# Post norms of a two-layer decoder trunk: sums of squares spread by a product with ones, roots computed on every partition

## The chip, the cores and the metric

The kernel runs on one core of one Trainium2 chip. A core has TensorE (PE in the profile, with its weight loads shown apart as PEld), VectorE (DVE), ScalarE (ACT), GpSimd (POOL) and SyncE (SP, which here only issues transfers). The metric is the time of one execution on the device in microseconds (us). The kernel before takes 1883.55 us, the median of three runs that lie between 1883.47 and 1885.15 us.

## The reference

The model is a trunk of two layers over 512 tokens and 16 meta tokens, 1024 features wide, in float32. Each layer is a half-step SwiGLU FFN, a token mixer (gated linear attention in layer 0, sliding-window attention in layer 1), and a second half-step FFN. After the first layer one set of keys and values is made. Every sub-layer is normed on both sides:

```python
def rmsnorm(x, g):
    xf = x.astype(jnp.float32)
    y = xf * lax.rsqrt(jnp.mean(xf * xf, axis=-1, keepdims=True) + EPS)
    return (y * g.astype(jnp.float32)).astype(x.dtype)
...
    h = h + 0.5 * rmsnorm(swiglu(rmsnorm(h, g[0]), w_ffn_in[layer, 0], w_ffn_out[layer, 0]), g[1])
...
    h = h + rmsnorm(mix, g[3])
    h = h + 0.5 * rmsnorm(swiglu(rmsnorm(h, g[4]), w_ffn_in[layer, 1], w_ffn_out[layer, 1]), g[5])
```

The outer `rmsnorm` of each line, the one whose result is added to `h`, is the post norm. It needs, for each token, the root of the mean square over the 1024 features of the sub-layer's output.

## The kernel before, in words

Features lie on partitions and tokens on the free axis: `H` (the residual stream) and `Y` (a sub-layer's output) are 128 partitions x 8 feature tiles x 528 tokens. So the sum of squares of a token runs over the 8 tiles, which ACT and POOL add up elementwise (`square_into`, L436), and over the 128 partitions, which PE sums.

Tokens go in two groups: 272 and 256 in layer 0, 256 and 256 in layer 1. At the end of a sub-layer (`out_steps`, L660) the output products of the first group are issued for all eight feature tiles m, then its norm is started as a job (L754, `finish.run`), then the output products of the second group follow, and then its norm. The next sub-layer begins with `x_first` (L607): 96 products on the first group's operand tiles (four weight units, eight feature tiles, three products each), then 96 on the second group's. PE therefore has the second group's output products while the first group is normed, and the first group's input products while the second group is normed.

The norm of a group is `Residual.run` (L505):

- After a delay, `rstd` (L419) is called with DVE as its engine. `root` (L362) multiplies the sums tile by a single column of ones, one small product for each chunk of tokens and each sums tile (L368): four chunks of 68 tokens for 272, two chunks of 128 for 256. There are one or two sums tiles: the default `parts=(1, 2)` gives one for the first group and two for the second, and `l1f1` (the norm after the attention of layer 1) has two for both. The sums then lie with tokens on partitions, 68 x 4 or 128 x 2.
- Ten small DVE instructions (L376 to L390) make the inverse root by a bit trick and two Newton-like steps.
- L423 puts the roots on a diagonal, `dg`, by a multiplication of the identity with the roots (68 x 272 or 128 x 256). After the planner's delay, L431 multiplies ones by `dg`, which brings each token's root to all partitions, in PSUM tile `r`.
- For each feature tile k, DVE computes `t = y * r` (L519) and `h = t + h` (L520), and `nxt.build` (L465) and `nxt.sumsq` make the next sub-layer's operand tile (ACT L470, DVE L471) and its squares. With 256 tokens `t` is the second half of `r`'s bank; with 272 it is a PSUM bank of its own for each k.

Where there is no next sub-layer (`out`), the first group goes to `store` (L526) and the second to `turn` (L542). The norms so treated are eleven: both groups of `l0m`, `l0f1`, `kv`, `l1m` and `l1f1`, and the first group of `out`. In the profile `l0f1` and `l1f1` appear as `l0f` and `l1f`, and `out`'s second group (`turn`) is `st_out`.

The order of PE's instructions is written by hand; that of the other engines is made by the compiler's scheduler from program order. The program order comes from a small planner (`Flow`, L72): its clock advances with each product by an estimate (L177), and jobs ask with `yield` for the time after which they go on. The constant `DCHAIN` (3.0) stands for the DVE chain between the sums' product and the spreading product. The pre norm of the next sub-layer (`Operand.factors`, L481) uses the same `rstd` with POOL as its engine, and is not touched.

Large SBUF tiles (weights after their split, operands, hidden tiles, scratch) share one pool of 32 pair slots (`pair_tile`, L158); small ones lie in pool `sm`; all PSUM tiles share eight banks.

Of the kernel before, what the change touches and what calls it, by code (L numbers as in the profile page):

```python
# [9 lines left out]
F32 = mybir.dt.float32  # L10
F32R = mybir.dt.float32r
I32 = mybir.dt.int32
AF = mybir.ActivationFunctionType
ALU = mybir.AluOpType
AX = mybir.AxisListType

P = 128
D = 1024
# [9 lines left out]
RSQRT_MAGIC = float(0x5F3759DF)  # L28
# [23 lines left out]
LOW = 1.0  # L52
SQUARED = 1.0
SCALED = 2.2
LAG = 5
PERIOD = 3.2
SLOWER = 4.0
# [78 lines left out]
def trunk_kernel(ctx: ExitStack, tc, a, out, last_out):  # L136
    nc = tc.nc
    pe, act, dve, pool, sp = nc.tensor, nc.scalar, nc.vector, nc.gpsimd, nc.sync
# [12 lines left out]
    ones = cp.tile([P, P], F32, name="ones")  # L151
# [3 lines left out]
    def ps(name):  # L155
        return pp.tile([P, 512], F32, tag="ps", name=name)

    def pair_tile(name, dt=F32R):  # L158
        return hp.tile([P, 2, TOK], dt, tag="pair", name=name)
# [5 lines left out]
    def flat(t):  # L165
        return t.rearrange("p a t -> p (a t)")
# [5 lines left out]
    def mm(o, lhs, rhs, start=True, stop=True, onto=False, cost=None):  # L172
        inst = pe.matmul(o, lhs, rhs, start=start, stop=stop, skip_group_check=onto)  # L173
        n = 1
        for d in rhs.shape[1:]:
            n *= d
        flow.clock += cost or (n / 2400 if rhs.dtype == F32R else max(n / 600, 0.12))  # L177
        return inst
# [36 lines left out]
    live, limit, room = [0], [16], [Job(None)]  # L215
# [187 lines left out]
    def half_roots(sums, dim, name):  # L403
# [12 lines left out]
        dve.scalar_tensor_tensor(yy, zz, 0.75, yy, op0=ALU.add, op1=ALU.mult)  # L416
        return yy

    def rstd(sq, n, dim, half, name, eng=pool, more=0.0):  # L419
        yy = root(sq, n, dim, name, eng, half=half)  # L420
        c, nch = yy.shape
        dg = sm.tile([P, 272], F32, tag="dg", name=f"dg_{name}", bufs=2)
        eng.tensor_tensor(  # L423
            dg[:c, :n].rearrange("p (j c) -> p j c", c=c),
            ident[:c, :c].unsqueeze(1).to_broadcast([c, nch, c]),
            yy.unsqueeze(2).to_broadcast([c, nch, c]),
            op=ALU.mult,
        )
        yield (DCHAIN if eng is dve else CHAIN) + more
        r = ps(f"r_{name}")  # L430
        mm(r[:, :n], ones[:c, :], dg[:c, :n])  # L431
        return r
# [18 lines left out]
    class Operand:  # L451
# [29 lines left out]
        def factors(self, gi, eng=pool):  # L481
            if self.column is not None:
                o, n = self.groups[gi]
                yield FACT + (ADDED if self.parts[gi] == 1 else 0)
                root(self.accs[gi], n, D, f"{self.name}_{o}", eng, *self.column[gi])
                yield CHAIN
                return
            if self.rt is None:
                self.rt = sm.tile([P, TOK], F32, tag="R", name=f"R_{self.name}", bufs=2)
            o, n = self.groups[gi]  # L490
            yield FACT + (ADDED if self.parts[gi] == 1 else 0)
            r = yield from rstd(self.accs[gi], n, D, False, f"{self.name}_{o}", eng, gi * BEHIND if eng is dve else self.more)
            act.activation(self.rt[:, o : o + n], r[:, :n], AF.Copy)
# [5 lines left out]
    class Residual:  # L499
# [5 lines left out]
        def run(self, gi, g, sums):  # L505
            o, n = g
            nxt = self.nxt
            if self.turned(gi):
                self.turn(g, sums)
                return  # L510
            yield 1.8 + (ADDED if self.parts[gi] == 1 else 0)
            r = yield from rstd(sums, n, D, self.half, f"post_{self.name}{gi}", dve)
            if nxt is None:
                yield from self.store(gi, g, r)
                return
            for k in range(KD):
                h, y = H[:, k, o : o + n], Y[:, k, o : o + n]
                t = r[:, 256 : 256 + n] if n <= 256 else ps(f"t_{self.name}{gi}{k}")[:, :n]
                dve.tensor_tensor(t, y, r[:, :n], op=ALU.mult)  # L519
                dve.tensor_tensor(h, t, h, op=ALU.add)  # L520
                nxt.build(gi, k)
                nxt.sumsq(gi, k)
                yield 1.0
            nxt.rjob[gi] = flow.spawn(nxt.factors(gi), gi * BEHIND)

        def store(self, gi, g, r):  # L526
            o, n = g
            rb = r[:, :n].unsqueeze(1).to_broadcast([P, 2, n])
            for k in range(0, KD, 2):
                h, y = H[:, k : k + 2, o : o + n], Y[:, k : k + 2, o : o + n]  # L530
                t = ps(f"t_{self.name}{gi}{k}").rearrange("p (k n) -> p k n", n=n)
                dve.tensor_tensor(t, y, rb, op=ALU.mult)
                dve.tensor_tensor(h, t, h, op=ALU.add)
                sp.dma_start(out[k : k + 2, :, o - META : o - META + n].rearrange("k p n -> p k n"), h)
                yield 1.0
# [46 lines left out]
    def x_units(x, nu, groups, evac):  # L582
        late = []

        def drain(i, g, p):
            for job in x.rjob:
                yield job
            evac(i, g, p)

        raw = x.column is not None  # L590

        for i in range(nu):
            w = next_w()
            pst = [ps(f"x{used[0]}_{gi}") for gi in range(len(groups))]
            for k in range(KD):
                for g, p in zip(groups, pst):
                    mm3(p[:, : g[1]], w, k, x.tiles[k], g, k == 0, k == KD - 1)
            done_w()
            for g, p in zip(groups, pst):
                if raw or all(job.done for job in x.rjob):  # L600
                    evac(i, g, p)
                else:
                    late.append(flow.spawn(drain(i, g, p)))
        return late
# [337 lines left out]
    def gla(x, finish):  # L942
        set_ahead(10)
        with tc.tile_pool(name="gp", bufs=1) as gp:
# [81 lines left out]
            def core(h, before):  # L1026
# [105 lines left out]
                act.activation(onm, pm[:META, :256], AF.Identity, scale=f[:META, 4:5])  # L1132
                yield SCALED
                pm = ps(f"pm{h}_t")
# [109 lines left out]
    def swa(x, kv, finish):  # L1244
        kz, vt, dv, vmz = kv
        cap[0] = used[0] + 8
        with tc.tile_pool(name="ap", bufs=1) as ap:
# [19 lines left out]
            def evac(u, g, p):  # L1267
                o, n = g
                if qd[u // 2] is None:
                    qd[u // 2] = pair_tile(f"q{u}", F32)  # L1270
                act.activation(qd[u // 2][:, u % 2, o : o + n], p[:, :n], AF.Copy, scale=0.125)
# [139 lines left out]
            def attend(i, *after_jobs):  # L1411
                wait = [*after_jobs, *paces[-1:]]
                softs.append(flow.spawn(soft(i, wait)))
                paces.append(flow.spawn(pace(i, wait)))
                cores.append(flow.spawn(core(i)))
# [4 lines left out]
            for i in range(8):  # L1420
                attend(i, turns[i // 4], *cores[max(i - LAG, 0) : max(i - LAG + 1, 0)])
            x_units(x, 4, L1W, lambda i, g, p: evac(4 + i, g, p))
# [3 lines left out]
            for i in range(8, 16):  # L1426
                attend(i, turned, cores[i - LAG])
            flow.wait(*cores[:4])
# [186 lines left out]
```

## Time and profile before

| what | value |
|---|---|
| median of three runs | 1883.55 us |
| time of the profiled execution | 1884.85 us |
| its span (first to last instruction) | 1883.1 us |
| granted TensorE clock | 0.999 |
| DVE busy | 1397.0 us (74%), 2829 instructions |
| ACT busy | 1026.3 us (54%), 2311 instructions |
| POOL busy | 164.0 us (9%), 297 instructions |
| DMA, mean | 93 GB/s |

Times are microseconds unless marked ns. L173 is the helper that issues all products, so product groups are told apart by tile names: `st_post_...` are the sums of a post norm, `r_post_...` its spread roots, `dg_post_...` the diagonal; the same names without `post` belong to the pre norms. A product in float32 shows as two records for each matmul. In a timeline row the columns are start, duration, engine, line, operation, output and inputs, shapes and count; the bracket gives how long the engine was idle before, and what it waited for. In the chain of work that ended last, a row is start, length and what it consists of.

### The profile page before, as it was taken

What the parts mean: (1) busy time and instruction counts of PE and PEld (TensorE: products, weight loads), DVE (VectorE), ACT (ScalarE), POOL (GpSimd) and SP (SyncE); (2) the same over time, 40 slices, a digit from 0 to 9 for tenths busy, and PEclk for the clock granted to TensorE, in tenths of its full rate; (3) what the DMA queues carried; (4) which work ended last, traced back from release to release, by engine and by line L of the source; (5) the groups of instructions that cost most, each with busy time, mean ns of one, the idle gap of its engine ahead of it and who ended that gap; (6) DMA issues with size and microseconds to landing.
All of it is one profiled execution on the core that took longest, in us unless ns stands there. A gap on an engine that the chain in (4) does not pass through costs nothing.

```text
span 1883.1 us, 37216 instructions
## 1 busy us (share of the span) xinstructions
PE 1865.4 (99%) x14453; PEld 1783.3 (95%) x14453; DVE 1397.0 (74%) x2829; ACT 1026.3 (54%) x2311; POOL 164.0 (9%) x297
## 2 busy tenths in 40 slices
PE   8999999999999999999999999999999999999998
PEld 8999999999999999999999898989987898989898
DVE  6885858767564788585888886868766779868685
ACT  5653535654446566363574553535757855636364
POOL 2000000230001300000033000000320140000002
PEclk9999999999999999999999999999999999999999
DMA  4333233421123123232351223233421212333331
GB/s 166 96 97 105 88 110 94 140 68 57 62 63 113 46 90 106 91 101 91 110 166 46 73 88 111 92 113 98 136 74 52 68 46 73 96 107 101 103 114 60
DMA packets 102273, 174.70 MB, mean 93 GB/s; under 512 B 11856, under 2 KB 24016, under 8 KB 102096
## 3 DMA queue, kind: packets, MB, share of 16 engines
q1 hardware_dynamic: 101520, 171.67, 29.0%
q8 instruction: 113, 1.85, 0.4%
q10 hardware_dynamic: 576, 0.65, 0.1%
q14 instruction: 64, 0.52, 0.1%
HBM read 169.66 MB, written 2.10 MB: 91 GB/s over the span
## 4 chain that ended last, share of the span: by engine, by line
PE 88%; DVE 7%; ACT 3%; issue 1%; DMA 0%; POOL 0%; SPq 0%; DVEq 0%; ACTq 0%; POOLq 0%
PE y L173 30%; PE a L173 19%; PE x L173 19%; PE c L173 8%; PE d L173 5%; DVE raw L262 1%; ACT w_s L256 1%; PE o L173 1%; DVE w_s L257 1%; PE e L173 1%; DVE w L257 1%; DVE w L238 1%; PE po L173 1%; ACT s L1348 0%; ACT Y L1348 0%
## 5 line engine op out<-in xcount | busy, mean ns | idle before, releaser
L257 DVE TENSOR_TENSOR w_s<-raw,w_s 128x512 fp32r<-128x512 f32 x288 | 193.9, 691 | 130.3 <-ACT w_s L256 128.7
L173 PE MATMUL y<-hidl0f,w 128*128 128x256 f32 (+1 forms) x2112 | 262.0, 285 | 1.1 <-DVE hidl0f L449 0.9
L173 PEld LDWEIGHTS y<-hidl0f,w 128*128 128x128 f32 x2112 | 259.0, 188 | 2.2 <-DVE hidl0f L449 1.5
L238 DVE TENSOR_TENSOR w<-raw,w 128x512 fp32r<-128x512 f32 x376 | 236.1, 659 | 30.7 <-ACT w L237 28.5
L256 ACT ACTIVATE w_s<-raw 128x512 fp32r<-128x512 f32 x288 | 175.1, 628 | 151.4 <-DVE raw L262 138.5
L173 PE MATMUL y<-hidl1f,w 128*128 128x512 f32 (+1 forms) x1344 | 251.1, 346 | 0.3 <-DVE hidl1f L935 0.2
L173 PEld LDWEIGHTS y<-hidl1f,w 128*128 128x128 f32 x1344 | 212.4, 188 | 35.1 <-DVE hidl1f L935 1.6
L237 ACT ACTIVATE w<-raw 128x512 fp32r<-128x512 f32 x376 | 206.4, 586 | 39.1 <-PE y L173 29.3
L262 DVE TENSOR_TENSOR raw<-raw,raw 128x512 f32<-128x512 f32 x288 | 198.3, 688 | 5.5
L444 POOL TENSOR_TENSOR acc_post<-acc_post,sq_post 128x256 f32<-128x256 f32 (+1 forms) x77 | 63.1, 820 | 1541.5 <-ACT sq_post L443 1540.7
L257 DVE TENSOR_TENSOR w<-raw,w 128x512 fp32r<-128x512 f32 x216 | 148.6, 688 | 29.9 <-ACT w L256 29.1
L256 ACT ACTIVATE w<-raw 128x512 fp32r<-128x512 f32 x216 | 134.0, 621 | 41.5 <-PE y L173 41.2
L173 PE MATMUL x<-x_l0m,w 128*128 128x272 f32 (+1 forms) x1152 | 152.1, 288 | 0.0
L173 PEld LDWEIGHTS x<-x_l0m,w 128*128 128x128 f32 x1152 | 143.4, 188 | 2.7 <-issue 1.7
L699 DVE TENSOR_TENSOR Y<-y,Y 128x256 f32<-128x256 f32 (+2 forms) x175 | 81.9, 474 | 71.9 <-PE y L173 71.4
L173 PE MATMUL a<-zl0f_t,w_s 128*128 128x264 f32 x864 | 117.2, 285 | 0.0
L173 PE MATMUL a<-zl1f_t,w_s 128*128 128x256 f32 x864 | 114.3, 281 | 0.8 <-ACT c L910 0.7
L173 PEld LDWEIGHTS a<-zl0f_t,w_s 128*128 128x128 f32 x864 | 110.0, 188 | 0.3
L173 PEld LDWEIGHTS a<-zl1f_t,w_s 128*128 128x128 f32 x864 | 107.3, 188 | 2.6 <-ACT c L910 2.3
L173 PE MATMUL x<-x_l0f,w 128*128 128x256 f32 (+1 forms) x768 | 99.4, 289 | 7.4 <-ACT w L237 6.2
L173 PEld LDWEIGHTS x<-x_l0f,w 128*128 128x128 f32 x768 | 96.3, 191 | 8.5 <-ACT w L237 6.2
L173 PE MATMUL x<-x_l1f,w 128*128 128x256 f32 (+1 forms) x576 | 93.0, 320 | 0.0
(514 smaller groups left out, 3215.7 us busy)
## 6 DMA issues: line engine op xcount, KB each, us to landing
raw<-in_w_in SPq DMA_DIRECT2D x352, 256.0 KB, 2.9
raw<-in_w_out SPq DMA_DIRECT2D x96, 256.0 KB, 3.3
raw<-in_w_last SPq DMA_DIRECT2D x48, 256.0 KB, 3.1
raw<-in_gla_in SPq DMA_DIRECT2D x48, 256.0 KB, 3.0
raw<-in_w_out SPq DMA_DIRECT2D x64, 128.0 KB, 2.9
raw<-in_gla_out SPq DMA_DIRECT2D x16, 256.0 KB, 2.8
raw<-in_w_q SPq DMA_DIRECT2D x16, 256.0 KB, 3.6
raw<-in_swa_out SPq DMA_DIRECT2D x16, 256.0 KB, 2.9
```

Of the source, the lines that this page charges most:

```text
L173: inst = pe.matmul(o, lhs, rhs, start=start, stop=stop, skip_group_check=onto)
L237: act.activation(w[:, 0, :m], raw[:, :m], AF.Copy)
L238: dve.tensor_tensor(w[:, 1, :m], raw[:, :m], w[:, 0, :m].bitcast(F32), op=ALU.subtract)
L256: act.activation(w[:, 0, :512], src, AF.Copy)
L257: dve.tensor_tensor(w[:, 1, :512], src, w[:, 0, :512].bitcast(F32), op=ALU.subtract)
L262: dve.tensor_tensor(dst, dst, src, op=ALU.add)
L444: pool.tensor_tensor(sums[0][:, :n], sums[0][:, :n], t[:, :n], op=ALU.add)
L699: dve.tensor_tensor(y, p[:, :n], y, op=ALU.add)
```

## The change

A new function, `spread`, takes the place of `rstd` in the post norms. It multiplies a full 128 x 128 tile of ones by each sums tile whole, so that the total of each token arrives on all 128 partitions at once. The ten DVE instructions then run on 128 partitions x 256 or 272 tokens instead of 128 x 2 or 68 x 4. The first writes back to the sums' PSUM bank `st`; the others use three stretches of a pair tile (`roots_...`) taken from the 32 slots. The diagonal and the product that spread it are gone. The sums' bank then serves as `t`, for 272 tokens too, and the roots are read from SBUF. The planner's delay for the chain is `SPREAD` (4.4) in the place of `DCHAIN` (3.0), and comes after the whole chain is issued.

```diff
+SPREAD = 4.4
...
+    def spread(sq, n, half, name):
+        st = ps(f"st_{name}")[:, :n]
+        for i, t in enumerate(sq):
+            mm(st, ones, t[:, :n], i == 0, i == len(sq) - 1)
+        room = flat(pair_tile(f"roots_{name}", F32))
+        yy, zz, ww = (room[:, i * 272 : i * 272 + n] for i in range(3))
+        last = (-0.25, 0.75) if half else (-0.5, 1.5)
+        dve.tensor_scalar(st, st, 1.0 / D, 1e-6, op0=ALU.mult, op1=ALU.add)
+        dve.tensor_scalar(yy.bitcast(I32), st.bitcast(I32), -0.5, RSQRT_MAGIC, op0=ALU.mult, op1=ALU.add)
+        dve.tensor_tensor(zz, yy, yy, op=ALU.mult)
+        dve.tensor_tensor(zz, zz, st, op=ALU.mult)
+        dve.tensor_scalar(ww, zz, 0.375, -1.25, op0=ALU.mult, op1=ALU.add)
+        dve.tensor_tensor(ww, ww, zz, op=ALU.mult)
+        dve.scalar_tensor_tensor(yy, ww, 1.875, yy, op0=ALU.add, op1=ALU.mult)
+        dve.tensor_tensor(zz, yy, yy, op=ALU.mult)
+        dve.scalar_tensor_tensor(zz, zz, last[0], st, op0=ALU.mult, op1=ALU.mult)
+        dve.scalar_tensor_tensor(yy, zz, last[1], yy, op0=ALU.add, op1=ALU.mult)
+        return yy, st
...
-            r = yield from rstd(sums, n, D, self.half, f"post_{self.name}{gi}", dve)
+            r, t = spread(sums, n, self.half, f"post_{self.name}{gi}")
+            yield SPREAD
...
-                t = r[:, 256 : 256 + n] if n <= 256 else ps(f"t_{self.name}{gi}{k}")[:, :n]
-                dve.tensor_tensor(t, y, r[:, :n], op=ALU.mult)
+                dve.tensor_tensor(t, y, r, op=ALU.mult)
...
-            rb = r[:, :n].unsqueeze(1).to_broadcast([P, 2, n])
+            rb = r.unsqueeze(1).to_broadcast([P, 2, n])
```

## The prediction

> **What bounds the kernel now.** I read the page first, then the list of who waited for whom on PE, then the chain of waits at the norms, then the DVE timeline there.
>
> ```profile
> span 1883.1 us, 37216 instructions
> ...
> PE 1865.4 (99%) x14453; PEld 1783.3 (95%) x14453; DVE 1397.0 (74%) x2829; ACT 1026.3 (54%) x2311; POOL 164.0 (9%) x297
> ...
> PE 88%; DVE 7%; ACT 3%; issue 1%; DMA 0%; POOL 0%; SPq 0%; DVEq 0%; ACTq 0%; POOLq 0%
> ```
>
> PE is idle for 18 us in 1883 and holds 88% of the chain. So time is won by giving PE less work, and lost wherever PE has to wait for an operand. The next list shows that a post norm hardly makes it wait so far:
>
> ```profile
> PE st_post_l1f L173 <- ACT acc_post L440: 0.9, 1, 0.9
> PE r_post_l1m L173 <- DVE dg_post_l1m L423: 0.7, 1, 0.7
> ```
>
> The chain of waits prices each piece of PE work in a norm. Columns: start, length, what.
>
> ```profile
> 362.01 0.43 PE st_post_l0m L173 x8
> ...
> 366.13 0.46 PE r_post_l0m L173 x2
> ...
> 986.56 0.79 PE st_post_kv L173 x8
> 987.35 1.62 PE x L173 x12
> ...
> 991.02 0.43 PE r_post_kv L173 x2
> ...
> 1860.05 0.34 PE st_post_out L173 x4
> ...
> 1864.04 0.43 PE r_post_out L173 x2
> ...
> 624.93 0.66 PE r_post_l0f L173 x2
> ```
>
> The reader sees that these pieces stand in PE's stream between dense products: PE pays for all of them.
>
> **The change part by part. PE.** The old spreading product has ones as weights and 256 or 272 columns in float32. The new sums' product has the same weights, size and type, so each costs what `r` costs: 0.43 us for 256, 0.46 for 272. With one sums tile the new product simply takes the place of `r`, and the small products go; with two, two new products stand against small ones and `r`.
>
> - First groups of 272, one tile (`l0m`, `l0f1`, `kv`): 3 x 0.43 = 1.3 us less.
> - First groups of 256, one tile (`l1m`, `out`): 2 x 0.34 = 0.7 us less.
> - Two tiles (the second groups of five norms, and the first of `l1f1`): 0.79 + 0.43 - 2 x 0.43 = 0.36 each, 6 x 0.36 = 2.1 us less.
>
> Together 4.1 us, all on PE's stream. I see no term of its own for the weights, since `r` has the same ones.
>
> Two waits for the diagonal go with it: 0.7 us at `l1m`, and 0.66 - 0.43 = 0.2 at `l0f1`: 0.9 us. The 0.9 us at `l1f1` is for squares that come late from ACT; I leave it where it is.
>
> **The DVE chain.** Before and after are to be compared from the sums' arrival to the first use of the root.
>
> ```profile
> 987.38 0.16 DVE L376 TENSOR_SCALAR av_post_kv<-st_post_kv 128x2 f32<-128x2 f32 x1 [0.29 <-PE st_post_kv L173]
> ...
> 989.42 0.43 DVE L423 TENSOR_TENSOR dg_post_kv<-ident,yv_post_kv 128x256 f32<-128x256 f32 x1
> 991.49 0.43 DVE L519 TENSOR_TENSOR r_post_kv<-Y,r_post_kv 128x256 f32<-128x256 f32 x1 [1.64 <-PE r_post_kv L173]
> 991.96 0.42 DVE L520 TENSOR_TENSOR H<-r_post_kv,H 128x256 f32<-128x256 f32 x1
> ```
>
> Before: 991.49 - 987.38 = 4.1 us, of which DVE waits 1.64 for the spread. After: ten wide instructions, one behind the other. No wide `TENSOR_SCALAR` of this kind is in the trace. From below each could cost the 0.16 us of L376, from above the 0.47 us from L519 to the dependent L520. I take 0.46 for all ten, since L519 and L520 have the width and either place of the operands: 4.6 us, and about 4.8 for 272. So a second group's root comes about 0.5 us later than before, not 2.5, because the trip over PE is saved. In return DVE is occupied all the time.
>
> In a first group the old chain shares DVE with the evictions of `y` and with POOL:
>
> ```profile
> 968.69 0.16 DVE L376 TENSOR_SCALAR av_post_kv<-st_post_kv 68x4 f32<-68x4 f32 x1
> 969.15 0.42 DVE L699 TENSOR_TENSOR Y<-y,Y 128x256 f32<-128x256 f32 x1
> ...
> 970.26 0.66 DVE L387 SCALAR_TENSOR_TENSOR yv_post_kv<-wv_post_kv,yv_post_kv 68x4 f32<-68x4 f32 x1
> ...
> 971.96 0.41 DVE L699 TENSOR_TENSOR Y<-y,Y 128x256 f32<-128x256 f32 x1
> 972.86 0.45 DVE L519 TENSOR_TENSOR t_kv<-Y,r_post_kv 128x272 f32<-128x272 f32 x1 [0.48 <-PE r_post_kv L173]
> ```
> ```profile
> 970.17 0.74 POOL L444 TENSOR_TENSOR acc_post<-acc_post,sq_post 128x256 f32<-128x256 f32 x1 [3.82 <-ACT sq_post L443]
> ```
>
> L387 takes 0.66 us where its neighbours take 0.16, and it ends with POOL's addition (970.17 + 0.74 = 970.91): a DVE instruction that comes during one waits it out. The Trainium skill (SBUF — State Buffer, Who interferes with whom) says that a DVE instruction with two SBUF inputs shares a read port with GpSimd, and whoever starts first holds it for the whole instruction; it speaks against a chain made ten times as wide, and the row agrees. I count one such hold of 0.5 us: 4.8 + 2 x 0.46 + 0.5 = 6.2 us against 972.86 - 968.69 = 4.2, so 2.0 us later. The cover is the second group's output products, which last until 982.43 in `kv` (row further down), so a first group's operands are still in time. But DVE passes on to the chain behind what it cannot make up: 0 to 1.5 us, as it is idle only 0.29 us ahead of `kv`'s second chain. I take the whole 1.5 at `kv`, 0.5 at `l1m` and nothing at `l1f1`.
>
> **Where PE will wait.** The second group's operands must be there when the first group's 96 input products are done, and PE now gets there 0.36 us sooner. The tightest places:
>
> ```profile
> 1365.31 0.15 DVE L376 TENSOR_SCALAR av_post_l1m<-st_post_l1m 128x2 f32<-128x2 f32 x1
> 1365.38 0.68 DVE L238 TENSOR_TENSOR w<-raw,w 128x512 fp32r<-128x512 f32 x1
> ...
> 1366.72 0.68 DVE L238 TENSOR_TENSOR w<-raw,w 128x512 fp32r<-128x512 f32 x1
> ...
> 1370.00 0.43 DVE L519 TENSOR_TENSOR r_post_l1m<-Y,r_post_l1m 128x256 f32<-128x256 f32 x1 [0.79 <-PE r_post_l1m L173]
> ...
> 1371.73 0.47 DVE L471 SCALAR_TENSOR_TENSOR x_l1m<-H,vec,x_l1m 128x256 fp32r<-128x256 f32 x1
> ...
> 1374.14 0.66 ACT L1271 ACTIVATE q<-x 128x256 f32<-128x256 f32 x2
> ```
> ```profile
> 1533.98 11.32 PE x L173 x96
> ```
> ```profile
> 1543.74 0.48 DVE L471 SCALAR_TENSOR_TENSOR x_l1f<-H,vec,x_l1f 128x256 fp32r<-128x256 f32 x1
> ```
>
> - `l1m`: ACT reads the first group's products at 1374.14, so PE turns to the second group about then. Its first operand is ready at 1372.20: 1.9 us to spare. After: PE comes 0.36 + 0.7 = 1.1 us sooner; three weight splits of 0.68 us stand in the chain (the first and the last above), and no idle time is left for them, so the operand comes 4.6 + 2.0 - (1370.00 - 1365.31) = 1.9 us later, and 0.5 more from the first group. PE waits 1.1 + 1.9 + 0.5 - 1.9 = 1.6 us.
> - `l1f1`: the last of the eight operands is ready at 1544.22, and PE needs it at 1533.98 + 7/8 x 11.32 = 1543.89: nothing to spare. 0.36 + 0.5 = 0.9 us of wait.
> - `kv`: rows below. At 991.46 there are 96 - 33 - 12 - 12 = 39 products of the first group left; at 7.37 / 60 = 0.123 us each PE reaches the second group at 996.3. The operand is ready at 993.79: 2.5 us to spare, of which 0.36 + 0.5 + 1.5 are used up. I allow 0.1 us for this and the two like it (`l0m`, `l0f1`), and up to 1 us each for the range.
>
> ```profile
> 982.43 4.13 PE x L173 x33
> ...
> 989.40 1.62 PE x L173 x12
> ...
> 991.46 7.37 PE x L173 x60
> ```
> ```profile
> 993.22 0.57 DVE L471 SCALAR_TENSOR_TENSOR x_kv<-H,vec,x_kv 128x256 fp32r<-128x256 f32 x1
> ```
>
> That makes 2.6 us of new waits; 0 if the scheduler puts the chain ahead of other DVE work, about 8 if it puts it behind.
>
> **Sum.** -4.1 - 0.9 + 2.6 = -2.4 us. The profiled execution takes 1884.85 us and its span 1883.1; it lies 1.3 us above the median of the three runs. So 1882.4 for an execution like it, and **1881.1** for the median.
>
> What I cost at nothing: `out`'s chain and store (DVE, hidden under the last output products); the roots read from SBUF instead of PSUM in L519 (one SBUF and one PSUM operand before, two SBUF operands after, exposed to POOL as above); the PSUM banks, of which the norm now needs one instead of one and eight passing ones.
>
> **The rivals.**
>
> *Full gain.* DVE's order adapts and PE never waits anew: -4.1 - 0.9 = -5.0, so 1878.5. For it: PE stands still for only 0.7 us at `l1m` today. Against it: the two places above are at their limit. Chance 0.25.
>
> *No change, through the pre norm.* POOL's root for the next operand runs beside the second group's chain, and wide DVE instructions hold it.
>
> ```profile
> 386.52 0.64 POOL L423 TENSOR_TENSOR dg_l0m<-ident,yv_l0m 68x272 f32<-68x272 f32 x1
> ...
> 389.46 0.62 PE L173 MATMUL r_l0m<-dg_l0m,ones 68*128 68x272 f32 x2
> ```
>
> Its diagonal is ready at 387.16, and PE asks for it at 389.46: 2.3 us to spare. Beyond that PE waits in order. If each of some ten POOL steps waited for one 0.46 us instruction, 4.6 us would be lost, 2.3 of them on PE; in one or two norms that eats the forecast's gain: about 1883.5. Against it: only part of POOL's root overlaps the chain. The Trainium skill (SBUF — State Buffer, Who interferes with whom) has the two sides block each other fully; it is the mechanism of this rival. Chance 0.1.
>
> *Slower, through the pair slots.* The chain's scratch comes from the 32 pair slots, and stays in use until the last k. Slots already run out:
>
> ```profile
> ACT w L256 <- PE y L173: 41.2, 26, 3.3
> ...
> ACT w L237 <- PE y L173: 29.3, 23, 2.2
> ```
>
> ACT waits for output products before it can write a split weight, up to 3.3 us at a time, because these free the slots. If the chain finds none, it waits as long; 3.3 + 0.9 us of delay against 1.9 to 2.5 to spare leaves 2 us of PE wait for each of five second groups: -5.0 + 10 = +5, so 1888.5. It decides the sign from 5 us of waits on. Against it: each output unit frees slots, and no wait of a norm's operand on a slot stands out in the trace. Chance 0.2.
>
> **How the numbers follow.** Forecast 0.45 (1880 to 1883.5 alone), full gain 0.25, pre norm 0.1, slots 0.2. 0.2% (3.8 us) is about what a measurement of this kernel can tell from no change: faster means under 1879.8, slower over 1887.3. The full gain falls below, and of the forecast a small part: 0.3. Of the slots' rival most lies above: 0.18. The rest, 0.52, is within. The range reaches from the full gain, 1878, to 1887, in the lower part of the slots' rival.
>
> **What would show it.** `st_post` pieces of 0.43 us for one tile and 0.86 for two, no `r_post`, no `dg_post`; ten chain instructions of about 0.42 us; PE's busy time some 4 us smaller; waits of PE on `x_l1m` and `x_l1f` of 1 to 2 us. Wrong would be: a wide float32 product that costs more than `r` did; PE waits at `l0m`, `l0f1` or `kv` of over 1 us; DVE or ACT waiting for a slot between a norm's sums and its chain; a changed order that moves time in the attention between 1390 and 1505 us, where I predict none.

## The result, and the profile after

The changed kernel takes 1899.44 us (median of five runs, 1898.76 to 1900.55) against 1883.55 us before: a ratio of 1.0082, with a 95% interval of 1.0071 to 1.0093. It is 15.9 us slower, where the prediction had 2.4 us faster. The profiled execution took 1899.72 us. In the changed kernel lines up to L418 stand one later than before, and those behind `spread` 21 later: the multiplication by the roots, L519, is L540; the addition L520 is L541; the operand's L471 is L492; GpSimd's addition L444 is L465; the eviction L699 is L720. The ten instructions of the wide chain are L428 to L437.

From the page of the changed kernel, the lines that answer to those shown of before:

```profile
span 1897.9 us, 37056 instructions
...
PE 1866.3 (98%) x14385; PEld 1780.6 (94%) x14385; DVE 1437.2 (76%) x2818; ACT 1028.7 (54%) x2311; POOL 175.6 (9%) x297
...
PE 72%; DVE 19%; ACT 5%; issue 2%; POOL 0%; DMA 0%; DVEq 0%; SPq 0%; POOLq 0%; ACTq 0%
```

PE is idle for 31.6 us instead of 17.7, its busy time has not fallen by the 4 us of the prediction, and DVE's share of the chain that ended last has gone from 7% to 19%. Whom PE waited for (us in total, times, longest):

```profile
PE x L174 <- ACT x_l0f L491: 2.6, 2, 2.0
PE x L174 <- ACT x_l0m L491: 2.4, 1, 2.4
...
PE x L174 <- DVE x_l1f L492: 1.7, 1, 1.7
PE x L174 <- ACT x_l1m L491: 1.5, 1, 1.5
PE x L174 <- ACT x_l1f L491: 1.4, 1, 1.4
```

All are operands of second groups, at `l0m`, `l0f1`, `l1m` and `l1f1`; together they are 9.6 us. The diagonals are gone from the list, as intended.

The granted TensorE clock adds to the two longest of these waits. It is 1.00 in nearly all of the trace, but 0.50 for 3.4 us from 403.3 us on, right behind the wait of 2.4 us at `l0m`, and for 3.4 us again from 638.8 us on, behind the one of 2.0 us at `l0f1`. Two windows at `l0m` (stretch, its length, PE's busy time and products, granted clock, DMA share, GB/s):

```profile
404.00:406.00 2.00, 2.00 (x12) 0.50 0.50 142
416.00:418.00 2.00, 2.00 (x19) 1.00 0.16 42
```

In the slow stretches the 128x256 products start every 0.213 us instead of every 0.118, and there are 16 of them in each: 16 x 0.095 = 1.5 us, 3.0 us together. PE counts as busy in them, which is part of the reason why its busy time has not fallen. The mean granted clock is 0.997 to 0.998 in all five executions, and 0.999 or 1.000 in nearly all of those of the kernel before; the profiled one of before has a single such stretch next to a norm, at 1505.9 us in `l1f1`. The waits of 1.4 to 1.7 us at `l1m` and `l1f1` are not followed by one. What a wait must be for it, no run here separates.

To see where the time came from, I take the first start of each norm's sums product (`st_post_...`) in the two traces. The difference from one to the next is what the stretch between them cost: the norm, and the products up to the next norm.

| stretch that begins with the norm | change's cost in the trace, us | predicted, us |
|---|---|---|
| before the first norm | +1.4 | 0 |
| `l0m` | +4.4 | -0.8 and some wait |
| `l0f1` | +4.6 | -1.0 and some wait |
| `kv` | +0.8 | -0.8 and some wait |
| `l1m` | +0.5 | -1.4 + 1.6 |
| `l1f1` | +2.6 | -0.7 + 0.9 |
| `out`, first group | +0.5 | -0.3 |

(The 1.4 us ahead of the first norm lie at the start of the program, before the first changed instruction. In the experiments below this stretch differs from before by -0.8 to +0.8 us.)

The cause shows in single instructions. First the kernel before, then the changed one, each beside two additions of GpSimd:

```profile
389.50 1.80 POOL L444 TENSOR_TENSOR acc_l0m<-acc_l0m,sq_l0m 128x256 f32<-128x256 f32 x2 [0.74 <-ACT sq_l0m L443]
389.73 0.42 DVE L519 TENSOR_TENSOR r_post_l0m<-Y,r_post_l0m 128x256 f32<-128x256 f32 x1
```
```profile
394.24 1.80 POOL L465 TENSOR_TENSOR acc_l0m<-acc_l0m,sq_l0m 128x256 f32<-128x256 f32 x2 [1.61 <-ACT sq_l0m L464]
394.49 0.97 DVE L540 TENSOR_TENSOR st_post_l0m<-Y,roots_post_l0m 128x256 f32<-128x256 f32 x1
395.38 0.95 DVE L492 SCALAR_TENSOR_TENSOR x_l0m<-H,vec,x_l0m 128x256 fp32r<-128x256 f32 x1
```

With the roots in PSUM the multiplication takes its 0.42 us in the middle of an addition (389.50 to 390.41). With the roots in SBUF it starts in the middle of one (394.24 to 395.17), and ends 0.3 us behind it: 0.97 us. This is no single case: of the 80 multiplications in the changed kernel, 37 start while a GpSimd instruction still runs for 0.1 us or more, and they take 0.72 us in the mean and up to 1.03; the other 43 take 0.43. Before, 47 start so, and none takes more than 0.44. The next instruction, the operand's L492, which had two SBUF operands before as well, is held by the second addition. The groups of all sixteen multiplications of a norm (busy time, mean ns), in the changed kernel:

```profile
L540 DVE TENSOR_TENSOR st_post_l0f<-Y,roots_post_l0f 128x272 f32<-128x272 f32 (+1 forms) x16 | 9.8, 610 | 0.3
...
L540 DVE TENSOR_TENSOR st_post_l1m<-Y,roots_post_l1m 128x256 f32<-128x256 f32 x16 | 9.3, 582 | 0.4
L540 DVE TENSOR_TENSOR st_post_kv<-Y,roots_post_kv 128x272 f32<-128x272 f32 (+1 forms) x16 | 9.2, 574 | 0.3
...
L540 DVE TENSOR_TENSOR st_post_l1f<-Y,roots_post_l1f 128x256 f32<-128x256 f32 x16 | 8.7, 542 | 0.2
L540 DVE TENSOR_TENSOR st_post_l0m<-Y,roots_post_l0m 128x272 f32<-128x272 f32 (+1 forms) x16 | 8.5, 534 | 0.3
```

and one of them before:

```profile
L519 DVE TENSOR_TENSOR r_post_l1m<-Y,r_post_l1m 128x256 f32<-128x256 f32 x16 | 6.8, 425 | 1.9 <-PE r_post_l1m L173 1.6
```

Together they take 45.5 us, where 80 at about 0.425 would take 34. What that does to a norm, at `l0m`'s second group in the changed kernel (DVE's timeline, then PE's):

```profile
384.57 0.42 DVE L428 TENSOR_SCALAR st_post_l0m<-st_post_l0m 128x256 f32<-128x256 f32 x1
...
389.02 0.43 DVE L540 TENSOR_TENSOR st_post_l0m<-Y,roots_post_l0m 128x256 f32<-128x256 f32 x1
...
405.20 0.95 DVE L492 SCALAR_TENSOR_TENSOR x_l0m<-H,vec,x_l0m 128x256 fp32r<-128x256 f32 x1
```
```profile
402.79 6.47 PE L174 MATMUL x<-x_l0m,w 128*128 128x256 f32 x39 [2.44 <-ACT x_l0m L491]
```

The chain itself is as predicted: 389.02 - 384.57 = 4.45 us for ten instructions (predicted 4.6). But DVE only gets to it at 384.57, because it is still busy with the first group, and from the first multiplication to the end of the last operand it needs 17 us.

### The profile page after: what moved, and what is told of

It is laid out like the page before. It is cut to its first block, busy times and chain, and to the rows that moved or that the text cites. A ratio compares the mean times of both kernels' runs of the same rounds, so it can differ in the third digit from the quotient of the medians.

```text
span 1897.9 us, 37056 instructions
## 1 busy us (share of the span) xinstructions
PE 1866.3 (98%) x14385; PEld 1780.6 (94%) x14385; DVE 1437.2 (76%) x2818; ACT 1028.7 (54%) x2311; POOL 175.6 (9%) x297
## 4 chain that ended last, share of the span: by engine, by line
PE 72%; DVE 19%; ACT 5%; issue 2%; POOL 0%; DMA 0%; DVEq 0%; SPq 0%; POOLq 0%; ACTq 0%
PE y L174 27%; PE a L174 17%; PE x L174 11%; PE c L174 7%; PE d L174 4%; DVE raw L263 2%; ACT w_s L257 2%; DVE w_s L258 2%; DVE w L258 2%; DVE H L541 1%; DVE w L239 1%; PE o L174 1%; PE e L174 1%; PE po L174 1%; DVE hidl1f L956 1%
## 5 line engine op out<-in xcount | busy, mean ns | idle before, releaser
L465 POOL TENSOR_TENSOR acc_post<-acc_post,sq_post 128x256 f32<-128x256 f32 (+1 forms) x77 | 65.9, 855 | 1530.6 <-ACT sq_post L464 1528.1
L720 DVE TENSOR_TENSOR Y<-y,Y 128x256 f32<-128x256 f32 (+2 forms) x175 | 81.7, 473 | 67.6 <-PE y L174 67.3
L174 PE MATMUL x<-x_l0f,w 128*128 128x256 f32 (+1 forms) x768 | 101.9, 293 | 11.1 <-ACT w L238 6.0
```

The costliest lines, as they stand in the source:

```text
L465: pool.tensor_tensor(sums[0][:, :n], sums[0][:, :n], t[:, :n], op=ALU.add)
L720: dve.tensor_tensor(y, p[:, :n], y, op=ALU.add)
```

## The experiments

**Theory P**: GpSimd's additions hold the DVE instructions that now read two SBUF operands, the 80 multiplications above all. **Theory Q**: the wide chain occupies DVE about 2 us longer per norm, and what follows is late for that. Times are medians; ratios are to the kernel before, run on the same chip, with a 95% interval. The experiments are numbered, and "the ninth kernel" is that of experiment 9. Times by stretch are taken as in the table above, against the kernel before.

**1. Roots back in PSUM.**

```diff
-        dve.scalar_tensor_tensor(yy, zz, last[1], yy, op0=ALU.add, op1=ALU.mult)
-        return yy, st
+        rr = bank[:, 256:512] if n <= 256 else ps(f"rr_{name}")[:, :n]
+        dve.scalar_tensor_tensor(rr, zz, last[1], yy, op0=ALU.add, op1=ALU.mult)
+        return rr, st
```

> The changed kernel, but the last instruction of the chain writes the roots to PSUM, so that the multiplication by the roots again reads one SBUF and one PSUM operand; nothing else differs. Theory P (the multiplication with two SBUF operands is held by GpSimd's additions: 80 of them took 45.5 us instead of 34.2): they fall back to 0.42-0.45 us each, 11 us of DVE go, and the kernel comes to 1886 to 1890 us. Theory Q (the wide chain keeps DVE occupied 2 us longer per norm, and later work of the norm is late for that): at most 3 us come back, 1896 us or more. If both share the loss: about 1892.

1892.04 us, ratio 1.0043 [1.0028, 1.0057]. Half comes back: the case of both sharing. But the edit also moved the order on DVE, which the compiler makes. At `l0m` in the changed kernel the evictions of the second group's `y` stand spread through the first group's chain (364.18, 366.30, 368.84 us); here all but the first stand behind it. DVE's timeline of this kernel, then PE's:

```profile
362.87 0.42 DVE L722 TENSOR_TENSOR Y<-y,Y 128x256 f32<-128x256 f32 x1
370.65 0.41 DVE L722 TENSOR_TENSOR Y<-y,Y 128x256 f32<-128x256 f32 x1
```
```profile
377.13 3.65 PE L174 MATMUL x<-x_l0m,w 128*128 128x272 f32 x27 [0.80 <-DVE Y L722]
381.23 0.70 PE L174 MATMUL st_post_l0m<-acc_post,ones 128*128 128x256 f32 x2 [0.44 <-POOL acc_post L467]
382.71 0.70 PE L174 MATMUL st_post_l0m<-acc_post,ones 128*128 128x256 f32 x2 [0.78 <-ACT acc_post L463]
```

For 7.8 us nothing is evicted; PE waits for an eviction and then for the late squares. It is the same at `kv` (7.9 us), but not in the other three norms, where the first group's chain keeps its order on DVE. By stretch this kernel costs +3.5 us at `l0m`, +0.4 at `l0f1`, +2.9 at `kv`, +0.1 at `l1m` and +0.2 at `l1f1`. So where the order stayed, the operand's place returns 4.2 us of 4.6 (`l0f1`) and 2.4 of 2.6 (`l1f1`), and what is left of the loss stands at the two norms whose order moved. The clock stays at 1.00 at all norms. The total of this run alone does not show one cost.

**2. A chain of seven instructions**, the last three left out.

```diff
         dve.scalar_tensor_tensor(yy, ww, 1.875, yy, op0=ALU.add, op1=ALU.mult)
-        dve.tensor_tensor(zz, yy, yy, op=ALU.mult)
-        dve.scalar_tensor_tensor(zz, zz, last[0], st, op0=ALU.mult, op1=ALU.mult)
-        dve.scalar_tensor_tensor(yy, zz, last[1], yy, op0=ALU.add, op1=ALU.mult)
```

> The changed kernel with the last three instructions of the chain left out (the last refinement of the root and its half step; so the roots are less exact, and twice as large where the step is a half). It takes 1.3 to 1.8 us of DVE from each of eleven norms and leaves the multiplication's operands in SBUF. Theory Q: a third or more of the loss comes back, 1890 to 1894 us. Theory P: the additions still hold the multiplication, 1896 us or more.

1884.41 us, ratio 1.0003 [0.9994, 1.0012]: 15 us come back, more than either theory had. With the total of the first run, this spoke for Q.

**3 and 4. Only the operand's place, in the kernel before.** ACT copies the spread roots, once to SBUF, once to PSUM, and L519 reads the copy.

```diff
+            rc = flat(pair_tile(f"rc_{self.name}{gi}", F32))[:, :n]    # 3
+            rc = ps(f"rc_{self.name}{gi}")[:, :n]                      # 4
+            act.activation(rc, r[:, :n], AF.Copy)
...
-                dve.tensor_tensor(t, y, r[:, :n], op=ALU.mult)
+                dve.tensor_tensor(t, y, rc, op=ALU.mult)
```

> The kernel before, with the spread roots copied by ACT from PSUM to SBUF, and the multiplication reading the copy. Compare with the next kernel, which has the same copy in PSUM. Theory P: 8 us or more slower than its twin, with multiplications of 0.8 to 1.0 us in the trace; the copy itself delays each norm by about 0.7 us and costs 0 to 4 us in both. Theory Q: the two within 2 us of each other.

> The kernel before, with the spread roots copied by ACT from PSUM to another PSUM bank, and the multiplication reading the copy: the cost of the copy alone. Both theories: 1883 to 1888 us, the multiplications at 0.42 to 0.45 us.

1895.78 us [1.0044, 1.0077] and 1892.94 us [1.0031, 1.0061]. The gap is 2.8 us, where P had 8 or more and Q less than 2. But the fourth kernel, expected at 1888 at most, is no clean control: it uses a bank more per norm, and PE waits for banks, as its list of waits shows:

```profile
PE r_kv L173 <- DVE r_post_kv L521: 2.9, 1, 2.9
PE r_l0f L173 <- DVE r_post_l0f L521: 1.9, 1, 1.9
```

**5 and 6. The pair again, without the further bank in most norms.** The copy goes to the free half of the roots' own bank, or to SBUF, and the product with `y` is written over the spread roots.

```diff
+            rc = r[:, 256:512] if n <= 256 else ps(f"rc_{self.name}{gi}")[:, :n]   # 5
+            rc = flat(pair_tile(f"rc_{self.name}{gi}", F32))[:, :n]                # 6
+            t = r[:, :n]
+            act.activation(rc, t, AF.Copy)
```

> The kernel before with the spread roots copied by ACT into the free half of their own bank (first groups of 272: another bank), and the product with y written over the spread roots. It is the copy without the further banks for which PE waited 4.8 us in the earlier one: the root comes about 0.7 us later and DVE has nothing more to do. If delay alone, without work on DVE, is absorbed: 1883 to 1885.5 us. If every delay of a root is paid on PE: 1888 us or more.

> As the kernel ahead of it, but with the copy in SBUF, so that the multiplication has two SBUF operands. Theory P: 5 to 9 us slower than its twin. Rival: within 2 us.

1884.76 us [0.9992, 1.0011] with the copy in PSUM, 1898.73 us [1.0065, 1.0095] with it in SBUF. A root that comes half a microsecond later (2.8 us of waiting for two groups of `l1m`, below, instead of the 1.9 above) costs nothing; an operand in SBUF costs 14.0 us, more than the 5 to 9 expected, in a kernel that has the old small chain. The multiplications of `l1m` (PSUM first, then SBUF):

```profile
L521 DVE TENSOR_TENSOR r_post_l1m<-Y,r_post_l1m 128x256 f32<-128x256 f32 x16 | 6.8, 425 | 2.8 <-ACT r_post_l1m L518 2.5
```
```profile
L521 DVE TENSOR_TENSOR r_post_l1m<-Y,rc_l1m 128x256 f32<-128x256 f32 x16 | 9.7, 604 | 2.8 <-ACT rc_l1m L518 2.6
```

The 14.0 us come near the whole loss of the change, but not by the same waits. In the sixth kernel PE waits for the old chain's diagonals and for GpSimd's sums, which are late as well:

```profile
PE r_post_l1m L173 <- DVE dg_post_l1m L423: 2.0, 1, 2.0
...
PE st_post_l0m L173 <- POOL acc_post L444: 1.6, 1, 1.6
```

The compiler's order on DVE and ACT is not quite the same in the two kernels, and the sixth has a stretch of 6.8 us at a clock of 0.50 in `kv`. So the pair shows that the operand's place is enough for a loss of this size, not how the change comes to its own.

**7 and 8. Without GpSimd's additions**, in the changed kernel and in the one before.

```diff
         act.activation(t[:, :n], src, AF.Square)
-        pool.tensor_tensor(sums[0][:, :n], sums[0][:, :n], t[:, :n], op=ALU.add)
```

> The changed kernel without GpSimd's additions of squares (the sums then hold the first, or the first and the last, of eight feature tiles only). If GpSimd's holds are half of the loss, as the roots in PSUM suggest, the gap to the next kernel is 6 to 9 us instead of 15.5. If holds are a small matter: 12 us or more. If they are all: under 3 us.

> The kernel before without GpSimd's additions of squares, as the level for the kernel ahead of it: 1880 to 1884 us, since PE hardly waits for the norms in it.

1879.98 us [0.9969, 0.9989] and 1882.26 us [0.9983, 1.0001]. PE's and DVE's instructions stand in the same order as with the additions, so this is the cleanest pair: the gap goes from +15.9 to -2.3 us. Nothing is left of the loss, with ten wide instructions in each chain and the roots in SBUF, and the clock is 1.00 at all norms of the seventh kernel. DVE's timeline at `l0m` in the changed kernel without additions, against the three rows above:

```profile
380.50 0.43 DVE L428 TENSOR_SCALAR st_post_l0m<-st_post_l0m 128x256 f32<-128x256 f32 x1 [0.49 <-PE st_post_l0m L174]
...
384.96 0.43 DVE L539 TENSOR_TENSOR st_post_l0m<-Y,roots_post_l0m 128x256 f32<-128x256 f32 x1
...
399.07 0.48 DVE L491 SCALAR_TENSOR_TENSOR x_l0m<-H,vec,x_l0m 128x256 fp32r<-128x256 f32 x1
```

The second chain is as long (4.46 us), but DVE now waits for its sums instead of the other way round, and the last operand is started 6.1 us earlier.

**9 and 10. A chain of seven that computes the whole root**, one cubic for the two steps; in the ninth kernel its last instruction also writes to PSUM, in the tenth to SBUF.

```diff
+WHOLE = (-0.6790226866358617, 2.853173295581011, 3.2278763388687777, 2.1893609583636646)
...
+        dve.scalar_tensor_tensor(zz, yy, kk, yy, op0=ALU.mult, op1=ALU.mult)
+        dve.tensor_tensor(zz, zz, st, op=ALU.mult)
+        dve.scalar_tensor_tensor(ww, zz, c1, zz, op0=ALU.add, op1=ALU.mult)
+        dve.scalar_tensor_tensor(ww, ww, c2, zz, op0=ALU.add, op1=ALU.mult)
+        dve.scalar_tensor_tensor(rr, ww, c3, yy, op0=ALU.add, op1=ALU.mult)
```

> The changed kernel with a chain of seven instructions instead of ten (one cubic in place of two steps, computing the same root) and with the last of them writing the roots to PSUM. If chain length and operand place are two separate costs (7.4 us came back by the one, 15.0 by the other), nothing of the loss is left and PE's smaller work shows: 1878 to 1881 us, faster than before. If both act on the same delay, and it is already used up by the shorter chain: 1882 to 1885 us.

> The changed kernel with the chain of seven instructions, roots in SBUF as in the change. Same count of instructions as the shortened chain of before (1884.41 us), but the whole root. If the number of wide instructions is what counts: 1883 to 1886 us. If the short chain was fast for another reason (the root of a refinement left out, other numbers): over 1890 us.

1881.64 us [0.9978, 0.9996] with the roots in PSUM: faster than before by 2.3 us, between the two cases expected, and the fastest version that leaves nothing out. It has the evictions behind the chain too, but goes without one for 5.0 us instead of 7.8 at `l0m`. With the roots in SBUF 1885.29 us [1.0001, 1.0019], as expected if the number of wide instructions counts. The short chain thus makes up for the holds almost entirely without removing them; the tenth kernel's multiplications are as slow as ever:

```profile
L540 DVE TENSOR_TENSOR st_post_l0m<-Y,roots_post_l0m 128x272 f32<-128x272 f32 (+1 forms) x16 | 9.9, 616 | 0.3
```

The page of the ninth, and its one large wait at a norm:

```profile
span 1879.9 us, 37043 instructions
...
PE 1860.0 (99%) x14385; PEld 1776.6 (95%) x14385; DVE 1407.1 (75%) x2785; ACT 1027.8 (55%) x2311; POOL 162.8 (9%) x297
```
```profile
PE x L176 <- DVE x_l1f L493: 1.6, 1, 1.6
```

By stretch it costs -0.8 (`l0m`), -0.9 (`l0f1`), -0.8 (`kv`), -1.2 (`l1m`), +0.7 (`l1f1`) and -0.5 us (`out`).

**11 and 12. The change in one group alone.**

```diff
+            if gi == 1:        # 11; gi == 0 in 12
+                r, t = spread(sums, n, self.half, f"post_{self.name}{gi}")
+                yield SPREAD
+            else:
+                bank = yield from rstd(sums, n, D, self.half, f"post_{self.name}{gi}", dve)
```

> The change in second groups alone; first groups (that of out among them) keep the diagonal and the spreading product. Theory D (a delay is paid on PE only beyond the slack, and the first group's delay is pushed into the second's): the slack takes part of the loss, and this and the next kernel together lose clearly less than 15 us: here 3 to 7 us over before. Rival E (every chain is paid where it stands): the two losses add up to 15 us, about 9 here.

> The change in first groups alone; second groups keep the diagonal and the spreading product. Theory D: -1 to +3 us against before, since the second group's output products cover it and its push falls into slack. Rival E: about +6 us.

1895.52 us [1.0049, 1.0077] and 1895.07 us [1.0045, 1.0073]: 11.6 and 11.1 us over before, 22.7 together. Both expectations fail: the halves lose more than the whole. In the twelfth the second group still needs its trip over PE, and its small chain is late behind the wide one on DVE. PE, whose order is fixed, stands there:

```profile
PE r_post_l0f L174 <- DVE dg_post_l0f L444: 4.4, 1, 4.4
PE r_post_kv L174 <- DVE dg_post_kv L444: 1.8, 1, 1.8
PE r_post_l1m L174 <- DVE dg_post_l1m L444: 1.7, 1, 1.7
```

It is a wait that the whole change does not have. In the eleventh PE waits for operands of second groups, as in the whole change: 2.5 us at `l0m` and 3.7 at `l1f1`. Why it loses so much there with the old chain in the first groups is not shown.

**13 and 14. Length against holds.** The ninth kernel with three more instructions in each chain, without use, once with one PSUM operand, once with two SBUF operands.

```diff
+        for _ in range(3):
+            dve.tensor_tensor(ww, zz, st, op=ALU.mult)    # 13; (ww, zz, yy) in 14
```

> The fastest version so far (chain of seven, roots in PSUM, 1881.64 us) with three further wide instructions in each chain, whose results are not used and which read one SBUF and one PSUM operand: ten instructions again, 1.4 us more of DVE in each of eleven norms, but no further one that GpSimd's additions can hold. If the holds decide and length alone is absorbed: 1881 to 1884 us. If the length of the chain decides: about 1891 to 1893, as with the chain of ten and roots in PSUM (1892.04 us).

> The same with the three further instructions reading two SBUF operands: the same length where nothing holds them, and open to holds. Both theories: 1888 to 1894 us; if the holds decide, at least 5 us over its twin; if the length decides, within 2 us of it.

1900.98 us [1.0073, 1.0103] and 1893.61 us [1.0032, 1.0066]. My expectation of the holds fails: the instructions with a PSUM operand cost 19 us over the ninth kernel, the others 12. And the others were hardly held (one of 33 took 0.98 us, the rest 0.41 to 0.44). So length does cost, in these versions. Both have the evictions behind the first group's chain at `l0m` and `kv`, as in the first run, and of the fourteenth's 12 us over the ninth, 8.4 lie in these two stretches. In the thirteenth PE waits long for squares; the second line is the same wait in the fourteenth:

```profile
PE st_post_l0f L176 <- ACT acc_post L464: 3.1, 1, 3.1
```
```profile
PE st_post_l0f L176 <- ACT acc_post L464: 0.6, 1, 0.6
```

Why the thirteenth loses 7.4 us more than the fourteenth, with the same order on PE and DVE, can be read from the stretches: all of it lies at `l0f1` (+4.2 against +0.6) and `l1f1` (+4.5 against +0.5), where the compiler's order on ACT differs. In the thirteenth the last square of `l0f1` starts on ACT at 627.72 us, in the fourteenth at 624.67; the last operand of `l1f1` makes PE wait 3.0 us in the thirteenth, and two operands 1.1 in the fourteenth. Behind these two waits, and behind one of 1.8 us for an eviction at `kv`, the thirteenth's clock is 0.50 for 3.4 us; the fourteenth's is 1.00 at all norms. So the pair compares two orders on ACT more than two kinds of instruction.

**15 and 16. The same question without the additions**, for the first kernel and the thirteenth.

> The changed kernel with the roots written to PSUM (1892.04 us), and without GpSimd's additions of squares; the order of PE's and DVE's instructions is the same as with them. If what was left of the loss are holds in the chain and in the operand's step: 1880 to 1882 us, as with the roots in SBUF and no additions (1879.98). If it is the other order on DVE, where the evictions of y stand behind the first group's chain: 1887 us or more.

> The version with the chain of seven, roots in PSUM and three further instructions of the kind that is not held (1900.98 us), without GpSimd's additions. If holds, 1880 to 1884 us. If order and length: 1893 us or more.

1884.46 us [0.9994, 1.0013] and 1890.08 us [1.0021, 1.0041], in the same order on PE and DVE as with the additions. The first kernel gains 7.6 us, the thirteenth 10.9: most of their loss goes with the additions. Not all of that need be holds, since without the additions the sums are ready sooner, and PE waited for late squares in both. But the first stays 4.5 us above the changed kernel without additions (1879.98), with as many instructions and nothing to hold them. Of this, 3.2 us lie at `l0m` and `kv`: the price of the order with the evictions behind the chain. Against the expectation, both causes have a part. Of the thirteenth's 6.5 us over before, 3.9 lie at `l1f1`, where its late operand on ACT makes PE wait 3.0 us as with the additions.

## Why the prediction was wrong, point by point

**PE's smaller work: right.** One tile costs 0.46 us at `l0m`, as predicted from `r`; the chain that ended last in the changed kernel has it:

```profile
363.32 0.46 PE st_post_l0m L174 x2
```

Where PE is not made to wait, the gain shows: `l0m` and `kv` cost -0.8 us each in the ninth kernel, as worked out (0.43 + 0.36), and PE's busy time falls by 1865.4 - 1860.0 = 5.4 us (predicted 4.1; the ends are modelled, and before has a slow stretch of the clock in it).

**The wait for the diagonal: right**, it is gone.

**The chain of ten: right in size.** A second group's takes 4.45 us at `l0m`, predicted as 4.6; the first groups' take 5.6 to 6.1, predicted as 6.2. The delay alone is absorbed: experiments 5 and 7. One reading in it was wrong: L519 and L520 do not stand for "either place of the operands", since both read one operand from PSUM.

**The step that failed** stands among the terms at nothing: "the roots read from SBUF instead of PSUM in L519 (one SBUF and one PSUM operand before, two SBUF operands after, exposed to POOL as above)". I had seen a hold of 0.5 us on L387, counted one per first group in the chain, and left the 80 multiplications at nothing, though they stand in the same loop in which GpSimd adds the squares. They cost 45.5 - 34 = 11 us of DVE, and the operands' L492 another 67.2 - 59.4 = 8 us (all 112 of them). The trace of before had the price in the same loop: L471, which reads two SBUF operands, takes 0.47 us at the least and up to 1.05, and L519 beside it never more than 0.45. The Trainium skill (SBUF — State Buffer, Who interferes with whom) says that a DVE instruction with at most one SBUF input, outside the two-port modes, does not contend with GpSimd, and one with two does, when GpSimd reads SBUF; the rows at 389.73 and 394.49 show both halves of that rule.

**The slack, second.** I gave `l0m`, `l0f1` and `kv` 0.1 us together, on 2.5 us to spare reckoned at `kv` for the first operand. They cost 9.8 us, and PE's waits at `l0m` and `l0f1` are over the 1 us that the prediction itself named as a sign of being wrong. Two errors: the last operand decides as much as the first, as eight operands have to keep up with PE; and a first group that is late pushes the second chain by far more than 0 to 1.5 us (the second chain at `l0m` starts 384.57 - 380.50 = 4.1 us later than without the holds, of which up to 1.4 lie in the start of the program). At `l1m`, where the sum had 1.6 us of wait, PE waits 1.5. The clock had no term: the two slow stretches behind the waits at `l0m` and `l0f1` make up about 3.0 us of the loss.

**Costs do not add up here.** The roots in PSUM return 7.4 us, three instructions less 14 to 15, no additions all of it: more than the loss. PE pays only for what exceeds the slack, so each remedy that brings DVE back below it returns most, and the slow clock goes with the long waits: the kernels of experiments 1, 2, 7, 9 and 10 have none of it before the end of the program. That is why the second experiment seemed to speak for the chain's length, and why experiments 7 and 8, whose order on PE and DVE is unchanged, are the ones that settle it.

**The rivals.** The pair slots were not it: ACT's waits for output products are as long as before,

```profile
ACT w L257 <- PE y L174: 41.0, 26, 3.3
...
ACT w L238 <- PE y L174: 29.4, 23, 2.2
```

and no chain waits for anything but its sums. The pre norm's wait is there, but small (in the changed kernel 0.8 us at `kv`). The full gain, 1878.5 us, is reached by no version that leaves nothing out. The ninth kernel comes to 1881.64 us, with 1.6 us lost at `l1f1`, where I had put 0.9. That it lies next to the 1881.1 of the prediction is chance: it is another kernel, with seven instructions and the roots in PSUM.

## What to carry to other kernels

When a change moves an operand from PSUM to SBUF, look at every instruction that reads it, not at the new ones only, and ask which GpSimd instruction with SBUF operands runs at that time: here such an instruction ended 0.2 to 0.3 us behind the addition in which it started. Where a loop keeps step with PE, reckon the slack at its last round, not at its first. When an experiment returns a loss, see whether the compiler's order stayed the same on every engine before giving its cause, and compare stretch by stretch. And look at the granted clock behind each long wait of PE: a wait can cost more than it lasts.

## What the runs showed of the hardware

A `TENSOR_SCALAR` with a single SBUF operand can be held as well. In the changed kernel L432 takes 0.28 to 0.30 us, but beside an addition that started 0.05 us ahead of it:

```profile
614.36 0.74 POOL L465 TENSOR_TENSOR acc_post<-acc_post,sq_post 128x256 f32<-128x256 f32 x1 [2.65 <-ACT sq_post L464]
614.41 0.84 DVE L432 TENSOR_SCALAR roots_post_l0f<-roots_post_l0f 128x272 f32<-128x272 f32 x1
```

The Trainium skill (SBUF — State Buffer, Who interferes with whom) has `tensor_scalar` among the operations that can enter a two-port mode and then contend; the row agrees, and the 0.30 us against 0.42 to 0.45 for the two `TENSOR_SCALAR` that read PSUM (L428 and L429) fit a faster mode. The hold works both ways: the additions' own median at `l0m` went from 0.84 to 0.93 us, and is 0.78 with the roots back in PSUM (experiment 1).
